# A decoder trunk on one core: its GEMM products read activations and write PSUM from the last column down, with row and weight splits placed anew by stage

## The chip, the cores and the metric

The kernel runs on one core of a Trainium2 chip. The metric is device time in microseconds (us) for one launch, as the median of the runs. Beside the runs there is one profiled execution, whose trace gives the start and the duration of every instruction on every engine: TensorE (PE, with weight loads as PEld), VectorE (DVE), ScalarE (ACT), GpSimd (POOL) and SyncE (SP).

## What is computed

The reference is a two-layer decoder trunk on 16 learned prefix tokens and 256 input tokens, so T = 272 columns of 2048 features, all in fp32:

```
h = concat(meta, x)                                   # 272 x 2048
a = rms_norm(h, norm_attn[0]);  q, k, v, f = split(a @ fox_w_in)
h = h + forgetting_attention(q, k, v, cumsum(log_sigmoid(f + b))) @ fox_w_o
h = h + square(relu(rms_norm(h, norm_mlp[0]) @ w_up[0])) @ w_down[0]
k, v = split(rms_norm(h, kv_norm) @ w_kv)             # layer 1 from here
q = rms_norm(h, norm_attn[1]) @ sb_w_q
h = h + stick_breaking_attention(q, k, v) @ sb_w_o
h = h + square(relu(rms_norm(h, norm_mlp[1]) @ w_up[1])) @ w_down[1]
return rms_norm(h, final_norm)[16:]
```

The MLPs are 2048 to 8192 to 2048. Of layer 1 only the 256 input tokens reach the output, so from its query projection on (the shared keys and values apart) the products need 256 columns and not 272.

## The kernel before, in words

Activations are held feature-major: features on the 128 partitions, 16 chunks of them, tokens along the columns. A product takes a 128x128 block of weights as the stationary operand and 272 or 256 columns of activations as the moving one, and adds to a PSUM tile `acc`.

To reach fp32 accuracy with the faster fp32r products, both operands are split into two fp32r parts, value = hi + lo, and each product is made three times: weight hi by row hi, weight hi by row lo, weight lo by row hi.

- `Split` (line 121) is the tile of one stage's split activations. A chunk has 640 elements per partition; hi and lo rows lie in it at two offsets taken from `ROWS` (line 27): 48 and 368 for 272 columns (t0 = 0), 0 and 320 for 256 columns (t0 = 16). Where t0 is not 0 it also defines `wide`, the hi rows with 6 columns more, and fills these with zeros by a POOL copy (line 135). ScalarE writes hi, VectorE lo (lines 137 to 142, 639 to 642).
- `weights` (line 201) loads a block of 512 output features by 512 input features in two DMAs of 512 KB on the SP queue, and splits it: ScalarE writes `whi` (line 225), VectorE `wlo` (line 226). Its argument `o1` is the element offset of the split weights in their tile, 0 for 272 columns and 16 for 256. The tiles hold 576 elements per chunk.
- `gemm_group` (line 230) makes 512 output features from all 2048 inputs: four weight blocks (kb), four input chunks in each (kc), four PSUM tiles (m) and three products: 192 products. `evac` then reads each PSUM tile. In `products` the 256-column order is pair, chunk, tile, the 272-column order tile, chunk, pair.
- In the 256-column stages three products of every fourth group (the list `wide`, line 261, with an own list for group 90) take `sp.wide`: 262 columns in place of 256, the 6 extra ones zero and never read.
- `gemm_matmul` (line 190) ties each product of the groups behind the one before it, so that the scheduler keeps their order.

The stages in order: 12 groups for q, k, v of layer 0 (`x_a0`), 4 for its output projection (`x_o0`), then four times 4 groups up (`x_m0`) and 4 groups down (`x_u0_f`); layer 1 has 4 groups for q (`x_a1`), 8 for keys and values (`x_kv`, 272 columns), 4 for the output projection (`x_o1`), and 16 up (`x_m1`) and 15 down (`x_u1_f`); the last block of 512 output features is made token-major by `token_group`, which the change does not touch. That is 56 groups at 272 columns and 39 at 256. Attention lies between the groups; its products (lines 435, 508, 603, 735, 757 and others) read some of the same splits (`x_o0`, `x_o1`) forward.

All tiles of splits begin at multiples of 64 elements.

Of the kernel before, what the change touches and what calls it, by code (L numbers as in the profile page):

```python
# [15 lines left out]
P = 128  # L16
D = 2048
NC = D // P
# [6 lines left out]
N_FF = 4  # L25

ROWS = {0: (48, 368), M: (0, 320)}
XROW = 640

G_A0, G_M0, G_KV, G_A1, G_M1, G_FIN = range(6)  # L30
# [3 lines left out]
def yoco_kernel(ctx: ExitStack, tc: tile.TileContext, hT_in, gains, b_f, w_f, w_qkv0, w_o0, w_up, w_dn,  # L34
                w_kv, w_q1, w_o1, g_row, out):
    nc = tc.nc
# [78 lines left out]
    pad = align.tile([P, 32], F32, name="pad")  # L115
# [5 lines left out]
    class Split:  # L121


        def __init__(self, label, t0):
            n = T - t0
            self.t0 = t0
            rows = xs.tile([P, NC * XROW + 64], F32R, tag="x", name=f"x_{label}")
            hi, lo = ROWS[t0]
            rows = rows[:, hi:hi + NC * XROW].rearrange("p (c t) -> p c t", c=NC)
            d = lo - hi  # L130
            self.hi, self.lo = rows[:, :, :n], rows[:, :, d:d + n]
            if t0:

                self.wide = rows[:, :, :n + 6]
                nc.gpsimd.tensor_copy(rows[:, :, n:n + 6], pad[:, :6].unsqueeze(1).to_broadcast([P, NC, 6]))

    def split_chunk(sp, gi, c):

# [47 lines left out]
    def behind(ins, other):  # L186
        tc.add_manual_dep(ins.ins, other.name, mybir.DependencyInfo(mybir.DependencyClass.NoSync,
                                                                    mybir.DependencyReason.DATA))

    def gemm_matmul(*args, **kw):  # L190

        ins = nc.tensor.matmul(*args, **kw).ins  # L192
        if queued and pinned[0]:
            tc.add_manual_dep(ins, queued[0].name, mybir.DependencyInfo(mybir.DependencyClass.NoSync,
                                                                        mybir.DependencyReason.DATA))
        queued[:] = [ins]
        if len(issued) == 192:
            issued.clear()
        issued.append(ins)

    def weights(u, kb, wblk, o1, load_x=None):

        src_w = wblk[kb].rearrange("p (k c) -> p k c", k=4)
        piece = 1 if load_x is not None and kb < 2 else 2
        raws = [wraw.tile([P, 2, 512], F32, tag="raw", name=f"raw_{u}_{kb}_{hf}") for hf in range(2)]
        for k0 in range(0, 4, piece):
            if load_x is not None:
                load_x(range(4 * kb + k0, 4 * kb + k0 + piece))
            if load_x is not None and kb == k0 == 0:

                for c0 in (0, 256):
                    nc.scalar.dma_start(raws[0][:, 0, c0:c0 + 256], src_w[:, 0, c0:c0 + 256])
            else:
                nc.sync.dma_start(raws[k0 // 2][:, k0 % 2:k0 % 2 + piece], src_w[:, k0:k0 + piece])
        parts = []
        for hf in range(2):
            whi, wlo = (wspl.tile([P, 2, 576], F32R, tag=f"w{x}", name=f"w{x}_{u}_{kb}_{hf}") for x in ("hi", "lo"))
            whi, wlo = whi[:, :, o1:o1 + 512], wlo[:, :, o1:o1 + 512]
            boxes = [(o, piece, 0, 512) for o in range(0, 2, piece)]
            if load_x is not None and kb == hf == 0:  # L220
                boxes[:1] = [(0, 1, 0, 256), (0, 1, 256, 512)]
            for o, no, c0, c1 in boxes:
                src = raws[hf][:, o:o + no, c0:c1]
                hp, lp = whi[:, o:o + no, c0:c1], wlo[:, o:o + no, c0:c1]
                on_act = nc.scalar.activation(hp, src, AF.Copy)  # L225
                on_dve = nc.vector.tensor_tensor(out=lp, in0=src, in1=hp.bitcast(F32), op=ALU.subtract)  # L226
            parts.append((whi, wlo))
        return parts, on_act, on_dve

    def gemm_group(wblk, sp, t0, evac, before={}, after={}, load_x=None):  # L230

        uid[0] += 1
        u = uid[0]
        accs = [pacc.tile([P, 512], F32, tag="acc", name=f"acc_{u}_{m}") for m in range(4)]
        n = T - t0
        for kb in range(4):
            if kb in before:
                before[kb]()  # L240
            parts, on_act, on_dve = weights(u, kb, wblk, 16 if t0 else 0, load_x)
            if kb in after:
                with tc.issue_after(on_act.ins), tc.issue_after(on_dve.ins):
                    after[kb]()

            if load_x is not None and kb == 0:
                runs = [([kc], range(4)) for kc in range(4)]
            elif kb in (0, 3):
                runs = [(range(4), [m]) for m in range(4)]
            else:  # L250
                runs = [(range(2 * hf, 2 * hf + 2), range(4)) for hf in range(2)]
            pinned[0] = load_x is None
            for kcs, ms in runs:
                pairs = ((0, sp.hi), (0, sp.lo), (1, sp.hi))
                if t0:
                    products = [(kc, m, *pair) for pair in pairs for kc in kcs for m in ms]
                else:
                    products = [(kc, m, *pair) for m in ms for kc in kcs for pair in pairs]
                left = {m: 3 * len(kcs) for m in ms}

                wide = [(0, 0, 0), (1, 0, 1), (2, 1, 1)] if t0 and u % 4 == 1 else []
                if u == 90:

                    wide = [(0, 0, 0), (0, 0, 1), (0, 2, 1)]
                for kc, m, part, x in products:
                    first, left[m] = kb == kc == 0 and left[m] == 3 * len(kcs), left[m] - 1
                    nw = n
                    if m == (0 if u == 90 else 3) and x is sp.hi and (kb, kc, part) in wide:
                        x, nw = sp.wide, n + 6
                    gemm_matmul(accs[m][:, :nw], parts[kc // 2][part][:, kc % 2, m * P:(m + 1) * P], x[:, 4 * kb + kc],  # L270
                                start=first, stop=kb == kc == 3 and left[m] == 0)
                if kb == 3:
                    for m in ms:
                        evac(m, accs[m][:, :n])
# [187 lines left out]
    for g in range(4):  # L462
# [11 lines left out]
        if g == 0:  # L474

            gemm_group(w_qkv0[0], xa, 0, lambda m, acc, qT=qT: nc.scalar.copy(qT[:, m, :], acc),
                       after={kb: (lambda kb=kb: first_norm(kb)) for kb in range(4)}, load_x=load_x)
# [12 lines left out]
        def decays(j):  # L490

            for i, (o, n) in enumerate(((0, 144), (144, T))):
# [5 lines left out]
                   after={j: (lambda j=j: decays(j)) for j in range(4)})  # L498
# [125 lines left out]
    def mlp(layer, xm, norm, t0, last_evac, last_group=None):  # L624
        box = {}

        def get_rstd():
            box["r"] = norm.finish()

        for f in range(N_FF):  # L630
            u = Split(f"u{layer}_{f}", t0)
            for g in range(4):
                def evac(m, acc, g=g):
                    c = 4 * g + m
                    r = tmp.tile([P, T], F32, tag="relu", name=f"relu_{layer}_{f}_{c}")
                    u2 = tmp.tile([P, T], F32, tag="u2", name=f"u2_{layer}_{f}_{c}")
                    nc.vector.scalar_tensor_tensor(out=r[:, t0:], in0=acc, scalar=0.0, in1=box["r"][:, t0:],
                                                   op0=ALU.max, op1=ALU.mult)
                    nc.scalar.activation(u2[:, t0:], r[:, t0:], AF.Square)
                    nc.scalar.activation(u.hi[:, c], u2[:, t0:], AF.Copy)  # L640
                    nc.vector.tensor_tensor(out=u.lo[:, c], in0=u2[:, t0:], in1=u.hi[:, c].bitcast(F32),
                                            op=ALU.subtract)
                gemm_group(w_up[layer, f, g], xm, t0, evac, {2: get_rstd} if f == g == 0 else {})
                if last_group is not None and f == N_FF - 1 and g == 0:
                    to_token_major()
            for g in range(4):
                def evac(m, acc, g=g):
                    residual_add(4 * g + m, acc, t0)
                    if f == N_FF - 1:
                        last_evac(4 * g + m)  # L650
                if last_group is not None and f == N_FF - 1 and g == 3:
                    last_group(w_dn[layer, f, g], u)
                else:
                    gemm_group(w_dn[layer, f, g], u, t0, evac)

    xm, norm_m = out_proj(w_o0, ao, 0, G_M0, "m0")
# [18 lines left out]
    for g in range(4):  # L675
# [4 lines left out]
        def split_c(kb, g=g):  # L680
            for c in ([4 * kb + g - 1] if g < 3 else [4 * kb + 2, 4 * kb + 3]):
# [3 lines left out]
                   after={kb: (lambda kb=kb: split_c(kb)) for kb in range(4)} if g else {})  # L685

    ao = Split("o1", M)
    for g in range(4):
# [12 lines left out]
        kc = packed(kT[:, :, 240:T], f"kc_{g}")  # L701
# [109 lines left out]
    xm, norm_m = out_proj(w_o1, ao, M, G_M1, "m1")  # L811
# [28 lines left out]
    def last_group(wblk, u):  # L840
        ob = xs.tile([P, NC * XROW + 64], F32, tag="x", name="ob")[:, :2 * D].rearrange("p (b d) -> p b d", b=2)

# [108 lines left out]
```

## Time and profile before

| what | value |
|---|---|
| median of 2 runs | 2282.02 us (2281.52 to 2282.51) |
| span of the profiled execution | 2278.5 us |
| median less span | 3.5 us |
| mean granted TensorE clock | 0.999 |
| TensorE products in the trace | 18,898 |
| data moved by DMA | 425.19 MB, 187 GB/s on average |

The profile gives for the profiled execution the span from its first to its last instruction; that is its own time here, and the runs' time lies 3.5 us above it. Products on TensorE overlap: one begins before the last one's modelled end. So a product's mean duration is no measure of what it costs; the distance between the starts of two products that follow each other is, and it is read off the timeline, where instructions of one kind that follow each other stand in one row with their count. A group of rows in the profile names line, engine, operation, the tile written and the tiles read, the shape, and the count. "wlo" and "whi" among the tiles read tell which part of the weights a product took.

### The profile page before, as it was taken

The page shows a single profiled execution, that of the slowest core. Times are in us where ns is not written, and L with a number is a line of the kernel's source. Part 1 is how long each engine was busy: PE and PEld are TensorE (multiplying, and loading weights), DVE is VectorE, ACT ScalarE, POOL GpSimd, SP SyncE. Part 2 cuts the span into 40 slices and gives each one's busy share as a digit, 9 for nine tenths or more (in the row PEclk, how much of TensorE's full clock was granted, in tenths as well). Part 3 has the DMA queues.
Part 4 walks back from the last instruction along what each step waited for, and adds up shares of the span by engine and source line. Part 5 has one row for each costly group of instructions (what it writes and reads, how often), then busy time and mean ns, then how long its engine had stood idle before and what let it go on. Part 6 is the DMA issues. An engine that isn't in the chain of part 4 may idle for free.

```text
span 2278.5 us, 44956 instructions
## 1 busy us (share of the span) xinstructions
PE 2271.1 (100%) x18898; PEld 2262.8 (99%) x18898; DVE 1333.5 (59%) x1930; ACT 1065.1 (47%) x1471; POOL 39.4 (2%) x72
## 2 busy tenths in 40 slices
PE   9999999999999999999999999999999999999998
PEld 9999999999999999999999999999999999999998
DVE  7767566554455455455566666666555555555555
ACT  6444445443354344335445555555443544543554
POOL 1000000000000000000000000000000000000001
PEclk9999999999999999999999999999999999999999
DMA  7765665555555555555556555555656556566564
GB/s 238 228 198 188 222 184 176 181 172 180 182 176 185 167 185 179 174 185 169 186 183 193 168 174 169 167 185 190 202 187 201 192 189 201 184 200 195 186 201 141
DMA packets 146171, 425.19 MB, mean 187 GB/s; under 512 B 31648, under 2 KB 43824, under 8 KB 145968
## 3 DMA queue, kind: packets, MB, share of 16 engines
q1 hardware_dynamic: 113760, 406.29, 54.1%
q10 hardware_dynamic: 32208, 16.02, 2.6%
q8 instruction: 148, 2.42, 0.4%
q14 instruction: 55, 0.45, 0.1%
HBM read 413.85 MB, written 8.41 MB: 185 GB/s over the span
## 4 chain that ended last, share of the span: by engine, by line
PE 99%; DMA 0%; issue 0%; POOL 0%; SPq 0%; POOLq 0%; ACT 0%; DVE 0%
PE acc L192 97%; PE po L435 0%; PE ps L435 0%; PE pza L435 0%; DMA raw<-w_qkv 0%; PE pzb L735 0%; PE po L804 0%; PE ps L508 0%; PE po L603 0%; PE pf L354 0%; PE pta L757 0%; PE pta L756 0%; PE pv L394 0%; POOL ob L850 0%; PE ptb L709 0%
## 5 line engine op out<-in xcount | busy, mean ns | idle before, releaser
L226 DVE TENSOR_TENSOR wlo<-raw,whi 128x1024 fp32r<-128x1024 f32 (+1 forms) x773 | 928.5, 1216 | 715.6 <-ACT whi L225 706.6
L225 ACT ACTIVATE whi<-raw 128x1024 fp32r<-128x1024 f32 (+1 forms) x773 | 796.4, 1050 | 961.0 <-PE acc L192 913.4
L192 PE MATMUL acc<-x_m,whi 128*128 128x272 f32 (+1 forms) x4096 | 643.1, 282 | 0.0
L192 PE MATMUL acc<-x_u,whi 128*128 128x272 f32 (+1 forms) x3968 | 626.0, 282 | 0.0
L192 PEld LDWEIGHTS acc<-x_m,whi 128*128 128x128 f32 x4096 | 566.0, 188 | 0.1
L192 PEld LDWEIGHTS acc<-x_u,whi 128*128 128x128 f32 x3968 | 550.4, 188 | 0.0
L192 PE MATMUL acc<-x_m,wlo 128*128 128x272 f32 (+1 forms) x2048 | 441.4, 282 | 0.0
L192 PE MATMUL acc<-x_u,wlo 128*128 128x272 f32 (+1 forms) x1984 | 432.1, 282 | 0.0
L192 PE MATMUL acc<-x_a,whi 128*128 128x272 f32 (+1 forms) x2048 | 355.4, 286 | 0.2 <-ACT whi L225 0.2
L192 PEld LDWEIGHTS acc<-x_m,wlo 128*128 128x128 f32 x2048 | 323.5, 188 | 0.0
L192 PEld LDWEIGHTS acc<-x_u,wlo 128*128 128x128 f32 x1984 | 315.3, 188 | 0.0
L192 PEld LDWEIGHTS acc<-x_a,whi 128*128 128x128 f32 x2048 | 301.3, 189 | 1.7 <-ACT whi L225 1.1
L192 PE MATMUL acc<-x_a,wlo 128*128 128x272 f32 (+1 forms) x1024 | 253.8, 286 | 0.0
L192 PE MATMUL acc<-x_kv,whi 128*128 128x272 f32 x1024 | 191.7, 288 | 0.0
L192 PEld LDWEIGHTS acc<-x_a,wlo 128*128 128x128 f32 x1024 | 175.7, 188 | 0.7 <-DVE ssq_a L158 0.4
L192 PE MATMUL acc<-x_o,whi 128*128 128x272 f32 (+1 forms) x1024 | 163.1, 283 | 0.0
L192 PEld LDWEIGHTS acc<-x_kv,whi 128*128 128x128 f32 x1024 | 160.1, 189 | 0.1
L192 PE MATMUL acc<-x_kv,wlo 128*128 128x272 f32 x512 | 147.6, 288 | 0.0
L192 PEld LDWEIGHTS acc<-x_o,whi 128*128 128x128 f32 x1024 | 142.3, 188 | 0.0
L307 DVE TENSOR_TENSOR hT<-acc,hT 128x272 f32<-128x272 f32 (+1 forms) x156 | 67.3, 431 | 75.4 <-PE acc L192 75.2
L192 PE MATMUL acc<-x_o,wlo 128*128 128x272 f32 (+1 forms) x512 | 110.7, 282 | 0.0
L192 PEld LDWEIGHTS acc<-x_kv,wlo 128*128 128x128 f32 x512 | 96.6, 189 | 0.0
(255 smaller groups left out, 1065.5 us busy)
## 6 DMA issues: line engine op xcount, KB each, us to landing
raw<-w_up SPq DMA_DIRECT2D x256, 512.0 KB, 3.9
raw<-w_dn SPq DMA_DIRECT2D x256, 512.0 KB, 4.0
raw<-w_qkv SPq DMA_DIRECT2D x92, 512.0 KB, 4.3
raw<-w_o SPq DMA_DIRECT2D x64, 512.0 KB, 3.9
raw<-w_kv SPq DMA_DIRECT2D x64, 512.0 KB, 4.4
raw<-w_q SPq DMA_DIRECT2D x32, 512.0 KB, 4.7
p_dram<-raw_p ACTq DMA_DIRECT2D x32, 96.0 KB, 4.6
v_dram<-turned ACTq DMA_DIRECT2D x48, 64.0 KB, 3.8
```

The costliest lines, as they stand in the source:

```text
L192: ins = nc.tensor.matmul(*args, **kw).ins
L225: on_act = nc.scalar.activation(hp, src, AF.Copy)
L226: on_dve = nc.vector.tensor_tensor(out=lp, in0=src, in1=hp.bitcast(F32), op=ALU.subtract)
L307: nc.vector.tensor_tensor(out=hT[:, c, t0:], in0=acc, in1=hT[:, c, t0:], op=ALU.add)
```

## The change

Three things are done, all in the products of `gemm_group` and in the places of their operands.

1. Every product of `gemm_group` reads its activation columns from the last to the first, and writes PSUM from the last column to the first. Each column's sum lands where it did. Weights are still loaded forward, and everything else reads and writes forward.
2. hi and lo rows of a stage lie at offsets of its own (`ROWS_OF`), and the weights of the up projections at 0, 16, 32 or 48 by the quarter f of the MLP. `x_m1` isn't in the table and keeps 0 and 320. The other weights keep 0 and 16.
3. The widened products and the zero fill of their extra columns are gone.

```diff
+ROWS_OF = {"a0": (0, 320), "o0": (16, 336), "m0": (32, 352), "u0_0": (0, 320), "u0_1": (0, 336), "u0_2": (0, 352),
+           "u0_3": (0, 368), "a1": (16, 336), "kv": (32, 368), "o1": (32, 352), "u1_0": (0, 320), "u1_1": (0, 336),
+           "u1_2": (0, 352), "u1_3": (0, 368)}
...
-            hi, lo = ROWS[t0]
+            hi, lo = ROWS_OF.get(label, ROWS[t0])
...
-            if t0:
-
-                self.wide = rows[:, :, :n + 6]
-                nc.gpsimd.tensor_copy(rows[:, :, n:n + 6], pad[:, :6].unsqueeze(1).to_broadcast([P, NC, 6]))
...
+    def backward(a):
+
+        *outer, (step, n) = a.ap
+        return bass.AP(a.tensor, a.offset + (n - 1) * step, [*outer, (-step, n)])
...
-    def gemm_group(wblk, sp, t0, evac, before={}, after={}, load_x=None):
+    def gemm_group(wblk, sp, t0, evac, before={}, after={}, load_x=None, shift=None):
...
-            parts, on_act, on_dve = weights(u, kb, wblk, 16 if t0 else 0, load_x)
+            parts, on_act, on_dve = weights(u, kb, wblk, shift if shift is not None else 16 if t0 else 0, load_x)
...
-                wide = [(0, 0, 0), (1, 0, 1), (2, 1, 1)] if t0 and u % 4 == 1 else []
-                if u == 90:
-
-                    wide = [(0, 0, 0), (0, 0, 1), (0, 2, 1)]
...
-                    nw = n
-                    if m == (0 if u == 90 else 3) and x is sp.hi and (kb, kc, part) in wide:
-                        x, nw = sp.wide, n + 6
-                    gemm_matmul(accs[m][:, :nw], parts[kc // 2][part][:, kc % 2, m * P:(m + 1) * P], x[:, 4 * kb + kc],
+                    gemm_matmul(backward(accs[m][:, :n]), parts[kc // 2][part][:, kc % 2, m * P:(m + 1) * P], backward(x[:, 4 * kb + kc]),
...
-                gemm_group(w_up[layer, f, g], xm, t0, evac, {2: get_rstd} if f == g == 0 else {})
+                gemm_group(w_up[layer, f, g], xm, t0, evac, {2: get_rstd} if f == g == 0 else {}, shift=16 * f)
```

## The prediction

> **What bounds the kernel now.** I read the page first: share of busy time, clock, and the chain that ended last.
>
> ```profile
> span 2278.5 us, 44956 instructions
> PE 2271.1 (100%) x18898; PEld 2262.8 (99%) x18898; DVE 1333.5 (59%) x1930; ACT 1065.1 (47%) x1471; POOL 39.4 (2%) x72
> PEclk9999999999999999999999999999999999999999
> PE 99%; DMA 0%; issue 0%; POOL 0%; SPq 0%; POOLq 0%; ACT 0%; DVE 0%
> ```
>
> TensorE is busy for all but 7 us at full clock, and the chain is 99% TensorE. The view of waits, for TensorE alone, says what it ever waited for:
>
> ```profile
> PE idle L61 <- DVE mean_w L57: 1.1, 1, 1.1
> PE pr_fin L192 <- DVE fin L863: 0.8, 1, 0.8
> PE acc L192 <- ACT whi L225: 0.2, 1, 0.2
> ```
>
> That is 2.1 us in all. So the time is the number of products times the distance from one product's start to the next: its pace. Durations (about 280 ns) overlap and say nothing here. The chain in order of time gives the pace of two long, undisturbed pieces:
>
> ```profile
> 427.93 756.83 PE acc L192 x6144
> 1581.78 533.37 PE acc L192 x4704
> ```
>
> The first piece is layer 0's MLP (272 columns): 756.83/6144 = 123.2 ns. The second is layer 1's MLP (256 columns): 533.37/4704 = 113.4 ns. The code has 56 groups of 192 products at 272 columns (10,752) and 39 at 256 (7,488, of which 33 are widened to 262, so 7,455). At these paces they make 1325 + 849 = 2174 us of the 2278.5. One nanosecond of pace is worth 10.8 us on the first kind and 7.5 us on the second.
>
> The pace isn't a constant of the shape. The timeline shows two values of it. First 256 columns, at the entry to three stages (query projection, output projection 1, MLP 1):
>
> ```profile
> 1186.94 1.11 PE L192 MATMUL acc<-x_a,wlo 128*128 128x256 f32 x8
> 1187.88 1.99 PE L192 MATMUL acc<-x_a,whi 128*128 128x256 f32 x16
> 1189.71 1.07 PE L192 MATMUL acc<-x_a,wlo 128*128 128x256 f32 x8
> 1190.62 1.07 PE L192 MATMUL acc<-x_a,whi 128*128 128x256 f32 x8
> ...
> 1493.99 2.05 PE L192 MATMUL acc<-x_o,whi 128*128 128x256 f32 x16
> 1495.88 1.11 PE L192 MATMUL acc<-x_o,wlo 128*128 128x256 f32 x8
> 1496.82 2.00 PE L192 MATMUL acc<-x_o,whi 128*128 128x256 f32 x16
> 1498.66 1.07 PE L192 MATMUL acc<-x_o,wlo 128*128 128x256 f32 x8
> 1499.57 0.62 PE L192 MATMUL acc<-x_o,whi 128*128 128x256 f32 x4
> ...
> 1583.50 1.11 PE L192 MATMUL acc<-x_m,wlo 128*128 128x256 f32 x8
> 1584.45 1.99 PE L192 MATMUL acc<-x_m,whi 128*128 128x256 f32 x16
> 1586.28 1.07 PE L192 MATMUL acc<-x_m,wlo 128*128 128x256 f32 x8
> 1587.18 1.07 PE L192 MATMUL acc<-x_m,whi 128*128 128x256 f32 x8
> ```
>
> Subtract starts. In the output projection, 24 products take 1496.82 - 1493.99 = 2.83 us, 117.9 ns each; the eight wlo products of the next turn take 1499.57 - 1498.66 = 0.91 us, 113.8 ns each. The other two stages do the same: eight in 0.94 and 0.95 us, then eight in 0.91 and 0.90 us. What lies at the switch? By form, the last stretch before it holds one widened product in each of the three stages:
>
> ```profile
> L192 PE MATMUL acc<-x_a,wlo 128*128 128x262 f32 x1 | 0.3, 284 | 0.0
> ...
> L192 PE MATMUL acc<-x_o,wlo 128*128 128x262 f32 x1 | 0.3, 283 | 0.0
> ...
> L192 PE MATMUL acc<-x_m,wlo 128*128 128x262 f32 x1 | 0.3, 285 | 0.0
> ```
>
> Nothing else differs in the code there. So at 256 columns the stream has a slow pace (117.9) that keeps itself up and a fast one (113.4) that does too, and a widened product seems to throw it from the one into the other: three stages of three. At 272 columns there are two paces as well; a stretch of the first products, then one of the MLP:
>
> ```profile
> 72.92 0.29 PE L192 MATMUL acc<-x_a,wlo 128*128 128x272 f32 x1
> ...
> 80.90 0.29 PE L192 MATMUL acc<-x_a,wlo 128*128 128x272 f32 x1
> ```
> ```profile
> 699.97 0.28 PE L192 MATMUL acc<-x_m,wlo 128*128 128x272 f32 x1
> ...
> 701.82 0.29 PE L192 MATMUL acc<-x_u,wlo 128*128 128x272 f32 x1
> ```
>
> A wlo product comes every third: 7.98 us for 63 products is 126.7 ns, 1.85 us for 15 is 123.3 ns. Here the slow pace ended without help.
>
> **The change part by part.** The instruction lists differ in nothing but seven POOL fills, the 33 products' width, and operands' addresses and direction: no instruction moves, no DMA or queue order changes, no wait is added.
>
> *Seven fills gone (line 135).* The pads of the widened products, on POOL:
>
> ```profile
> L135 POOL CAST x_u<-pad 128x96 fp32r<-128x96 f32 x4 | 1.1, 267 | 612.1 <-PE acc L192 612.1
> L135 POOL CAST x_m<-pad 128x96 fp32r<-128x96 f32 x1 | 0.5, 482 | 26.1 <-PE acc L192 26.1
> ```
>
> Under half a microsecond each, on an engine that is busy 2% and 0% of the chain: nothing. Without that cover all seven would be about 2 us.
>
> *Widened products gone.* Directly this saves 33 x 6 columns; at 113.4/256 = 0.44 ns a column, 0.1 us. Indirectly it removes what ended the slow pace. If layer 1's stages enter slow as they do now and nothing ends it, 7,455 products pay 117.9 - 113.4 = 4.5 ns: +33.5 us. If reading backward has no such slow pace: 0. Those are the ends. I take +33.5, since three entries of three were slow and each ended only with a widened product.
>
> *Other places of rows and weights.* Splits (ScalarE hi, VectorE lo) write as many elements at another offset. The weight splits already run at offset 0 in layer 0 and 16 in layer 1, with the same mean (first row from 500 to 1100 us, second from 1600 to 2200 us):
>
> ```profile
> L226 DVE TENSOR_TENSOR wlo<-raw,whi 128x1024 fp32r<-128x1024 f32 x203 | 245.1, 1223 | 244.9 <-ACT whi L225 244.9
> ...
> L226 DVE TENSOR_TENSOR wlo<-raw,whi 128x1024 fp32r<-128x1024 f32 x221 | 265.8, 1223 | 203.3 <-ACT whi L225 198.6
> ```
>
> So nothing, under TensorE's cover; eight of them are 9.8 us in a group that takes TensorE 192 x 113.4 = 21.8 us. For the products it may matter. Every stride between chunks is a multiple of 64 elements, so what a placement sets is the offset modulo 64. Now weights lie 16 elements past the rows in both shapes: rows 48, weights 0 at 272 columns; 0 and 16 at 256. The change gives 272 columns distances of 0 (qkv), -16 (output projection), -32 (kv) and -32 to 16 (up), and lets hi and lo part by up to 48 in the down projections. Only 4 of 56 groups keep the old distance, and 19 of 39 at 256 columns (by hi). No row shows a group at another distance, so the price goes by the two paces: between 0 and 126.7 - 123.3 = 3.4 ns on 10,752 products, +36.6 us; a gain is not excluded, since nobody's distance need be the best. I take 0, the row of most groups: the slow stretch at 272 columns ended by itself.
>
> *Backward.* Rows are read, and PSUM written, from the last column down; weights still load forward. No row of the trace has a negative step. Bounds: below, the closest thing to a stream limited by weight loads alone, the closing products of 128 columns:
>
> ```profile
> 2269.18 2.62 PE L192 MATMUL idle_fin<-mean_w 128*128 128x128 f32 x22
> ```
>
> The last lasts 0.275, so 21 starts in 2.345 us: 111.7 ns. At 256 columns that is -1.7 ns, -12.7 us. At 272 the shape has no lower row than 113.4 of the narrower one: -9.9 ns, -106 us. Above, both slow paces: +70 us together, already counted. I take 0 for the direction itself, in the middle, as the same columns stream.
>
> Sum against the profiled execution: 2278.5 - 0.1 + 33.5 = 2312 us of span. The runs' median is 2282.02, 3.5 us over the span, so 2315 us (+1.5%).
>
> **The rivals.**
> *B, the change does nothing to the pace*: descending order has one pace, and each stage stays at 123.3 and 113.4. Against it: the same instruction has two paces in this trace. For it: both values are locked over hundreds of microseconds. 2282 us. [...]
>
> *C, slow everywhere*: the scattered distances put 272 columns at 126.7 too. For it: a slow stretch of 63 products exists at the old distance. Against: it ended. 2315 + 36.6 = 2352 us (+3.0%). It passes 2% (about what a measurement of this kernel can tell from no change; 45.6 us) from a third of the 272-column products on, (45.6 - 33)/36.6.
>
> *D, faster*: moving rows and weights pass each other in opposite directions, so that they never run side by side and both slow and fast pace give way to a shorter one. It decides at a pace of 119.1 ns at 272 columns (45.6 us/10,752 = 4.2 ns off 123.3) with 256 unchanged. Bounds 2282 - 106 - 13 = 2163 us; halfway 2222. For it: 272 columns cost 9.8 ns more than 256, though 16 columns at 0.44 are 7.1, so there's slack of 2.7 ns at least. Against: no row shows it.
>
> *E, descending access isn't streamed at full rate*: at half rate all GEMM products double, some +2100 us. No row speaks to it; all operands there step forward by one. [...]
>
> **How the numbers follow.** A (2315) 0.34, B (2282) 0.13, C (2352) 0.29, D (2222) 0.17, E (over 4000) 0.07. Within 2%: A and B, 0.47. Slower: C and E, 0.36. Faster: D, 0.17. The likeliest case alone spans 2282 to 2328. For 8 in 10 I leave out E and the lower part of D: from 2220 to 2362 us, the top being C with 10 us for places worse than either pace.
>
> **What would show it.** In the changed profile: starts of wlo products in layer 1's long piece near 117.9 ns (A, C) or 113.4 (B); in layer 0's near 123.3 (A, B), 126.7 (C) or under 119 (D); differences between the four up projections of one layer would show that the places matter, none that only direction does. TensorE's waits should stay about 2 us. I am wrong if they grow, if a pace lies outside 111.7 to 117.9 at 256 columns or 113.4 to 126.7 at 272, or if the clock row falls below 9.

## The result and the profile after

The changed kernel takes 2332.7 us (median; 2332.16 to 2333.25) against 2282.02: 1.0226 times as long, interval 1.0207 to 1.0245. The span of its profiled execution is 2331.5 us, 53.0 more than before. The prediction said 2315, in a range of 2220 to 2362.

The page, same lines as before:

```profile
span 2331.5 us, 44923 instructions
PE 2322.9 (100%) x18898; PEld 2314.3 (99%) x18898; DVE 1335.5 (57%) x1930; ACT 1065.6 (46%) x1471; POOL 36.5 (2%) x65
PEclk9999999999999999999999999999999999999999
PE 99%; DMA 0%; issue 0%; POOL 0%; DVE 0%; SPq 0%; ACT 0%; POOLq 0%; ACTq 0%
```

TensorE makes as many products and is busy 51.8 us longer (2322.9 less 2271.1), at the same clock (1.000 on average against 0.999); VectorE and ScalarE are busy as long as before, within 2 us (1335.5 against 1333.5, 1065.6 against 1065.1). Its waits (engine, line, what it waited for, us in total):

```profile
PE idle L64 <- DVE mean_w L60: 1.1, 1, 1.1
PE pom L575 <- ACT vm_sb L573: 1.1, 1, 1.1
PE pr_fin L196 <- DVE fin L860: 0.8, 1, 0.8
PE acc L196 <- ACT whi L229: 0.4, 1, 0.4
```

That is 3.4 us in all, one wait of 1.1 us more than before. So it isn't waits that cost 53 us; the products follow each other more slowly. The chain in order of time (start, length, products), first three pieces of before that the prediction doesn't show, then the same five stretches after:

```profile
1185.22 104.29 PE acc L192 x899
1493.92 87.43 PE acc L192 x770
...
2116.02 138.64 PE acc L192 x1187
```
```profile
431.21 766.17 PE acc L196 x6144
1197.85 107.77 PE acc L196 x899
1511.76 92.23 PE acc L196 x770
1604.42 556.93 PE acc L196 x4704
2162.22 145.38 PE acc L196 x1187
```

Layer 0's MLP (x6144, 272 columns) grew by 766.17 - 756.83 = 9.3 us. The other four, mostly of 256 columns, grew by 3.5 + 4.8 + 23.6 + 6.7 = 38.6 us. The rest of the 53.0 lies in the shorter pieces between. Within one piece the pace isn't one number. The view by windows, for the GEMM line alone, with a window inside each of the four up projections of layer 0 and then of layer 1 (x counts the products; two of them began before the window):

```profile
445.00:510.00 65.00, 65.00 (x520) 1.00 0.55 179
613.00:703.00 90.00, 90.00 (x726) 1.00 0.57 182
805.00:895.00 90.00, 90.00 (x725) 1.00 0.56 182
997.00:1087.00 90.00, 90.00 (x722) 1.00 0.57 182
1618.00:1680.00 62.00, 62.00 (x527) 1.00 0.61 195
1777.00:1860.00 83.00, 83.00 (x707) 1.00 0.61 194
1960.00:2043.00 83.00, 83.00 (x694) 1.00 0.60 189
2187.00:2229.00 42.00, 42.00 (x352) 1.00 0.60 192
```

Length by count less two: 125.5, 124.3, 124.5 and 125.0 ns in layer 0, 118.1, 117.7, 119.9 and 120.0 ns in layer 1. The four stages of a layer run the same code and differ in the weights' offset only. So the places do matter, and none of these stages is at 123.3 or 113.3 any more.

### The profile page after: what moved, and what is told of

It reads as the page before. It is cut to its first block, busy times and chain, and to the rows that moved or that the text cites. A ratio compares the mean times of both kernels' runs of the same rounds, so it can differ in the third digit from the quotient of the medians.

```text
span 2331.5 us, 44923 instructions
## 1 busy us (share of the span) xinstructions
PE 2322.9 (100%) x18898; PEld 2314.3 (99%) x18898; DVE 1335.5 (57%) x1930; ACT 1065.6 (46%) x1471; POOL 36.5 (2%) x65
## 4 chain that ended last, share of the span: by engine, by line
PE 99%; DMA 0%; issue 0%; POOL 0%; DVE 0%; SPq 0%; ACT 0%; POOLq 0%; ACTq 0%
PE acc L196 96%; PE po L432 0%; PE ps L432 0%; PE pza L432 0%; DMA raw<-w_qkv 0%; PE pzb L732 0%; PE po L801 0%; PE ps L505 0%; PE po L600 0%; PE pf L351 0%; DMA v_dram<-turned 0%; PE pta L754 0%; PE pta L753 0%; PE pv L391 0%; POOL ob L847 0%
## 5 line engine op out<-in xcount | busy, mean ns | idle before, releaser
L196 PE MATMUL acc<-x_m,whi 128*128 128x272 f32 (+1 forms) x4096 | 659.1, 285 | 0.0
L196 PE MATMUL acc<-x_u,whi 128*128 128x272 f32 (+1 forms) x3968 | 639.7, 285 | 0.0
L196 PEld LDWEIGHTS acc<-x_m,whi 128*128 128x128 f32 x4096 | 577.5, 188 | 0.1
L196 PEld LDWEIGHTS acc<-x_u,whi 128*128 128x128 f32 x3968 | 559.3, 188 | 0.0
L196 PE MATMUL acc<-x_m,wlo 128*128 128x272 f32 (+1 forms) x2048 | 448.7, 285 | 0.0
L196 PE MATMUL acc<-x_u,wlo 128*128 128x272 f32 (+1 forms) x1984 | 437.4, 285 | 0.0
```

## The experiments

Three theories were set against each other. P: at 256 columns there are two self-sustaining paces, and the widened products end the slow one. D: falling access costs by itself. O: what counts is the distance of rows and weights. For D two halves were told apart later: R, the order in which rows are read, and W, the order in which PSUM is written. In the diffs, `...` marks lines not shown. The kernel before, run beside the experiments, had medians of 2280.6 to 2280.7 us; ratios are against these runs.

**Widened products and their fills taken out, nothing else.**

```diff
-            if t0:
-
-                self.wide = rows[:, :, :n + 6]
-                nc.gpsimd.tensor_copy(rows[:, :, n:n + 6], pad[:, :6].unsqueeze(1).to_broadcast([P, NC, 6]))
...
-                wide = [(0, 0, 0), (1, 0, 1), (2, 1, 1)] if t0 and u % 4 == 1 else []
...
+                wide = []
...
```

> The kernel before without its 33 widened products and their zero fills; forward, old places. Theory P (two self-sustaining paces at 256 columns, and a widened product is what ends the slow one): the 256-column stages stay at 117.9 ns from their entry on, 272 columns stay at 123.3; about +33 us, 2315. Theory D (descending access costs, widening is idle): 113.4 and 123.3 stay, 2282. Theory O (the distance of rows and weights costs): 2282.

2286.46 us, 1.0024 times before (1.0013 to 1.0035): +5.9 us and not +33. The chain:

```profile
428.31 756.82 PE acc L188 x6144
1185.59 107.15 PE acc L188 x899
1497.17 90.69 PE acc L188 x770
1588.29 533.14 PE acc L188 x4704
```

The pieces of the query projection (107.15 against 104.29) and of the output projection (90.69 against 87.43) are slow in all their 256-column products: 90.69/770 is 117.8 ns. P is right there. But MLP 1 (533.14) is as fast as before with no widened product in it. What ends the slow pace there is a break in its first group, where the norm's two products (line 159 here) come in between; ahead of it:

```profile
1586.75 1.10 PE L188 MATMUL acc<-x_m,wlo 128*128 128x256 f32 x8
1587.69 0.59 PE L159 MATMUL pms_m<-ssq_m,mean_w 128*128 128x256 f32 x2
```

Eight products take 0.94 us, 117.5 ns; behind the break the piece of 4,704 has 113.3. In the kernel before, the stream came to this break fast (eight wlo products from 1580.27 us on in 0.91 us, 113.8 ns) and left it slow (15 products from 1581.73 on in 1.77 us, 117.8 ns), and was fast again behind a widened product (eight in 0.90 us, in the prediction's rows). So one and the same break left the stream fast in one kernel and slow in the other. The norm's two products are one of plain fp32 in the code; they take 0.43 us of the chain of before, where an fp32r product takes 0.113 to 0.118:

```profile
1581.35 0.43 PE pms_m L163 x2
```

The prediction's other slow stretches of the kernel before also begin behind a break, and none of them where its stage begins. Ahead of the query projection's break the kernel before is fast:

```profile
1183.69 1.07 PE L192 MATMUL acc<-x_a,wlo 128*128 128x256 f32 x8
1184.60 0.62 PE L163 MATMUL pms_a<-ssq_a,mean_w 128*128 128x272 f32 x2
```

Eight products take 0.91 us, 113.8 ns each; behind the break come the prediction's 117.9. In the output projection the attention's products (lines 394, 435, 802 and 804) are the break: ahead of them 19 products from 1484.04 us on take 2.16 us, 113.7 ns, behind them eight from 1489.07 on take 0.94 us, 117.5 ns. At 272 columns, too, the slow stretch from 69 to 81 us begins behind two attention products (line 435, at 69.00; the three products from 68.50 on still take 0.37 us, 123.3 ns each) and ends at two others:

```profile
81.41 0.27 PE L552 MATMUL pm<-ident,s 128*128 128x128 f32 x1
81.51 0.27 PE L553 MATMUL pm<-ident,pk_sm 128*128 128x128 f32 x1
...
81.88 0.29 PE L192 MATMUL acc<-x_a,wlo 128*128 128x272 f32 x1
...
82.25 0.29 PE L192 MATMUL acc<-x_a,wlo 128*128 128x272 f32 x1
```

From one of these wlo rows to the next three products take 0.37 us, 123.3 ns each. So that pace didn't end without help, as the prediction has it: a break ended it.

**Backward at the old places.**

```diff
-            hi, lo = ROWS_OF.get(label, ROWS[t0])
+            hi, lo = ROWS[t0]
...
-                gemm_group(w_up[layer, f, g], xm, t0, evac, {2: get_rstd} if f == g == 0 else {}, shift=16 * f)
+                gemm_group(w_up[layer, f, g], xm, t0, evac, {2: get_rstd} if f == g == 0 else {})
```

> The changed kernel with the old places: backward, no widened products. Theory P: 256 columns at 117.9, 272 columns at 123.3, 2315. Theory D: as the changed kernel, 118 to 120 and 124.4 to 125.4, about 2333. Theory O: 113.4 and 123.3, 2282.

2329.03 us, 1.0210 (1.0180 to 1.0240).

```profile
431.54 767.31 PE acc L196 x6144
...
1604.62 554.03 PE acc L196 x4704
```

767.31/6144 = 124.9 ns, 554.03/4704 = 117.8 ns, the same in nearly all groups of a width. Against the run without widened products (2286.46) direction alone costs 42.6 us. D holds: it alone comes near at both widths. O falls as the sole cause, and P's 123.3 at 272 columns fails.

**Backward at the old places, widened products kept.**

```diff
-                    gemm_matmul(accs[m][:, :nw], parts[kc // 2][part][:, kc % 2, m * P:(m + 1) * P], x[:, 4 * kb + kc],
+                    gemm_matmul(backward(accs[m][:, :nw]), parts[kc // 2][part][:, kc % 2, m * P:(m + 1) * P], backward(x[:, 4 * kb + kc]),
```

> The kernel before with rows read and PSUM written backward, old places, widened products kept (the six zero columns come first). Theory P: the widened products end the slow pace here too, 113.4 after each; 2282 if direction is free. Theory D: 256 columns stay at 118 or above and 272 at 124.4 or above in spite of them, about 2333. Theory O: 2282.

2329.77 us, 1.0213 (1.0184 to 1.0243).

```profile
431.95 767.32 PE acc L197 x6144
...
1605.11 554.07 PE acc L197 x4704
```

The 33 widened products change nothing (2329.77 against 2329.03 us), and P's 113.4 behind each of them fails. Read backward, the stream has, as far as these runs go, one pace at this distance: 117.8 ns at 256 columns, the number of the slow one forward, and 125.0 at 272 through the stretch from 69 to 81 us too, where the forward stream is at 126.7. So P's two paces are seen in the forward read alone.

**The new places, forward, without and with widened products.** The first is the changed kernel with `backward` left out; the second is the kernel before with the table of places and the weights' offsets.

```diff
-                    gemm_matmul(backward(accs[m][:, :n]), parts[kc // 2][part][:, kc % 2, m * P:(m + 1) * P], backward(x[:, 4 * kb + kc]),
+                    gemm_matmul(accs[m][:, :n], parts[kc // 2][part][:, kc % 2, m * P:(m + 1) * P], x[:, 4 * kb + kc],
```

> The changed kernel reading and writing forward: new places, no widened products. Theory P: 256 columns at 117.9 in every stage, 272 at 123.3, 2315. Theory D: 2282 and no stage off its old pace. Theory O: paces that differ by stage, 118 to 120 and 124 to 126 where the distance is not the old one; about 2333, and the old paces where it is (up projections of the last quarter in layer 0, of the second in layer 1).

> Forward, the new places, widened products kept. Theory P (two self-sustaining paces at 256 columns where weights lie 16 elements past the rows): the down projections of the first quarter and the up projections of the second in layer 1, at 117.8 without widened products, come to 113.33 with them; the other stages, at other distances, stay as they were without; about 7 us under the run of places alone, some 2329. If the widened products do nothing for them: 2336.

2336.26 us, 1.0242 (1.0212 to 1.0271), and 2329.76 us, 1.0215 (1.0186 to 1.0245). Places alone cost about as much as direction alone (2336.26 and 2329.03 us), and the two don't add: both together are the changed kernel, 2332.70. The widened products are worth 6.5 us here, as P had it, and it lies in the two MLP stages of layer 1 where hi and lo are both at distance 16 (weights' offset less rows' offset). In layer 1's down projection of the first quarter, without them and with them:

```profile
1699.99 2.05 PE L196 MATMUL acc<-x_u,whi 128*128 128x256 f32 x16
1701.88 1.10 PE L196 MATMUL acc<-x_u,wlo 128*128 128x256 f32 x8
1702.82 0.40 PE L196 MATMUL acc<-x_u,whi 128*128 128x256 f32 x2
```
```profile
1699.95 1.98 PE L195 MATMUL acc<-x_u,whi 128*128 128x256 f32 x16
1701.77 1.07 PE L195 MATMUL acc<-x_u,wlo 128*128 128x256 f32 x8
1702.67 0.50 PE L195 MATMUL acc<-x_u,whi 128*128 128x256 f32 x3
```

24 products take 2.83 us (117.9 ns) and 2.72 us (113.3 ns), at the same places and in the same direction. This is the cleanest sight of the two paces. Both streams enter the stage slow; by the starts in the trace, the second turns from 117.8 to 113.3 ns right behind its first product of 262 columns, at 1695.84 us.

These runs, with the kernel before, the changed kernel and the backward ones, also give the pace by distance (taken modulo 64 elements). The numbers are mean times in ns from one start to the next, over undisturbed groups behind a stage's first one, hi and lo at equal offsets:

| distance | 272 forward | 272 backward | 256 forward | 256 backward |
|---|---|---|---|---|
| 16 | 123.33 (126.67 in the stretch at 69 us) | 125.00 | 113.33 or 117.78 | 117.78 |
| 0 | 125.33 | 124.44 | 120.00 | 118.33 |
| 32 | 126.67 | 125.33 | 118.67 | 120.00 |
| 48 | 126.67 | 124.44 | 117.78 | 120.00 |

Where a distance occurs at two places, the pace is the same: at 272 columns 16 with rows 48 and weights 0, and with rows 32 and weights 48; at 256 columns 0 with both at 0 and both at 16, in either direction. O is right in that distance and direction set the pace together. No cell is under the fast one of the kernel before. The cells of 126.67 may be a second pace that was entered, as is seen for distance 14 below; no run tells for these.

The table holds only where hi and lo lie at equal distances. Where they don't, the pace needn't be a mean of the two cells: layer 0's down projection of the third quarter (hi at 0, lo at 32) runs forward at 124.44 ns, below both, and that of the second quarter (hi at 0, lo at 48) backward at 125.19, above both. Why is open.

**Only the read, only the write backward.** Two kernels at the old places, without widened products: one has `backward` around the rows alone, the other around PSUM alone. Each product's columns land in reversed order, so neither computes the reference; number and shape of the products are the same. The first one's edit, against the changed kernel:

```diff
-                    gemm_matmul(backward(accs[m][:, :n]), parts[kc // 2][part][:, kc % 2, m * P:(m + 1) * P], backward(x[:, 4 * kb + kc]),
+                    gemm_matmul(accs[m][:, :n], parts[kc // 2][part][:, kc % 2, m * P:(m + 1) * P], backward(x[:, 4 * kb + kc]),
```

> As the backward kernel at the old places without widened products, but only the rows are read from the last column; PSUM is written forward, so each product's columns land in reversed order and the output is another one. Theory R (the order in which rows are read against the weight loads sets the pace): 125.0 ns at 272 and 117.8 at 256 columns, about 2329. Theory W (the falling order of PSUM writes costs): 123.33 and 113.33 with the first two 256-column stages at 117.8, about 2286.

> The counterpart: rows are read forward and only PSUM is written from the last column, so each product's columns land in reversed order and the output is another one. Theory R: 123.33 and 113.33, with the query and output projection of layer 1 at 117.8, about 2286. Theory W: 125.0 and 117.8, about 2329.

2329.23 us, 1.0213 (1.0183 to 1.0243), for the read; 2287.01 us, 1.0027 (1.0016 to 1.0038), for the write. The two long pieces, read then write:

```profile
432.29 767.31 PE acc L196 x6144
...
1605.38 554.03 PE acc L196 x4704
```
```profile
428.65 756.82 PE acc L196 x6144
...
1588.62 533.14 PE acc L196 x4704
```

The first has the pieces of the wholly backward run to the last digit, the second those of the forward run without widened products. R is shown, at these places: all of it is the reading of rows; writing PSUM in falling order costs nothing that can be seen (2287.01 against 2286.46 us).

**Order of blocks, order inside blocks.** Old places, no widened products, rows and PSUM in blocks of 16 columns (64 bytes).

```diff
-        return bass.AP(a.tensor, a.offset + (n - 1) * step, [*outer, (-step, n)])
+        return bass.AP(a.tensor, a.offset + n - 16, [*outer, (-16, n // 16), (1, 16)])
```

and `a.offset + 15, [*outer, (16, n // 16), (-1, 16)]` for the other.

> Old places, no widened products; rows are read and PSUM is written in blocks of 16 columns, the blocks from the last to the first, the columns inside a block rising. Theory B (what counts is the order in which the read passes blocks of 64 bytes while weights load): as wholly backward, 125.0 and 117.8, about 2329. Theory I (falling order of single elements counts): as forward without widened products, 123.33 and 113.33 but for the query and output projection of layer 1, about 2286. Any other pace: the two-step pattern has a price of its own.

> The counterpart: blocks of 16 columns from the first to the last, the columns inside a block falling. Theory B: as forward without widened products, about 2286. Theory I: as wholly backward, about 2329.

2369.98 us, 1.0390 (1.0360 to 1.0421), for falling blocks; 2606.17 us, 1.1426 (1.1393 to 1.1459), for falling columns inside rising blocks. The long pieces of the one and of the other:

```profile
443.26 790.82 PE acc L196 x6144
...
1645.54 554.03 PE acc L196 x4704
```
```profile
478.74 859.52 PE acc L196 x6144
...
1790.94 627.19 PE acc L196 x4704
```

Falling blocks give 117.8 ns at 256 columns, as wholly backward, but 128.7 at 272; falling columns in rising blocks 133.3 and 139.9. Neither theory has these: the two-step pattern has prices of its own, so the pair doesn't settle which order the direction works through. Nor does it tell whether the prices lie in the read or in the write, as both take the pattern here.

**Finer distances.** The kernel before with other weights' offsets in the MLPs, in two runs: up projections 8, 12, 20, 24 and down projections 4, 28, 14, 18 by quarter; then up projections 20, 24, 14, 18 and every down projection at 16.

```diff
+            self.first = hi
...
-            parts, on_act, on_dve = weights(u, kb, wblk, 16 if t0 else 0, load_x)
+            parts, on_act, on_dve = weights(u, kb, wblk, (sp.first + far) % 64, load_x)
...
```

> The kernel before (forward, widened products) with distances between 16 and its neighbours on the grid of 16 elements: up projections 8, 12, 20, 24 by quarter, down projections 4, 28, 14, 18. Theory O (pace is a function of direction and of the distance of rows and weights modulo 64): each value has one pace for its width, the same in all four groups of the stage; those near 16 at 123.33 and 113.33, those near 0 and 32 at 125.3 and 118 to 120. If only blocks of 16 elements count, 20 and 24 go with 16; if there is a better place than 16, a pace under 123.33 or 113.33 shows it.

> The kernel before with up projections at distances 20, 24, 14, 18 by quarter and every down projection at 16. If 126.67 at 272 columns with 20 and 14 was carried over from the stage ahead (28), then 20 and 14 come to 123.33 here, as 18 and 24 did; if the distance sets it, they stay at 126.67 and each down projection is at 123.33 again. Layer 1: 118.7, 118.7, 117.8 and 118.3 as seen for these distances, and 113.33 for each down projection after its first widened products.

2323.92 us, 1.0190 (1.0160 to 1.0219), and 2298.92 us, 1.0079 (1.0050 to 1.0108). At 256 columns the paces went from 117.8 (14) and 118.3 (4, 8, 12, 18) over 118.7 (20, 24) to 120.0 (28); the four distances that both runs have agree within 0.2 ns, and only 16 gave 113.33. At 272 columns 12 gave 124.44; 18 and 24 gave 123.33 in both runs and 20 gave 126.67 in both, so the carrying over that was offered for 20 falls: in the second run the stage ahead ends at 123.3. O's two paces near 16 (123.33 and 113.33) are thus met in part only. For 14 the carrying over holds: a window inside its stage, first run, then second:

```profile
920.00:990.00 70.00, 70.00 (x555) 1.00 0.53 175
```
```profile
815.00:885.00 70.00, 70.00 (x570) 1.00 0.57 179
```

70 us by 553 and by 568 products (the counts less the two that began before): 126.6 and 123.2 ns. At this distance, too, 272 columns have two paces. No finer distance beats 16.

**Nine widened products in place of 33.** In the first group of the query projection, the output projection and MLP 1 only.

```diff
-                wide = [(0, 0, 0), (1, 0, 1), (2, 1, 1)] if t0 and u % 4 == 1 else []
...
+                wide = [(0, 0, 0), (1, 0, 1), (2, 1, 1)] if u in (49, 61, 65) else []
...
```

> The kernel before with widened products only in the first group of the query projection, of the output projection and of the MLP of layer 1 (nine in place of 33). Theory P (a pace keeps itself up once it's entered): 113.33 from there to the end, the same time as before, 2282. If each stage needs its own: 117.8 in later stages, up to 2305.

2280.13 us, 1.0000 (0.9988 to 1.0011), and the long piece of MLP 1:

```profile
1581.84 533.25 PE acc L192 x4704
```

As expected from P: the fast pace, once entered, lasts 533 us without help. No run of this case beat the kernel before beyond its interval.

## Why the prediction held in its number and not in its cause

The median lies 18 us over the forecast, and that nearness is luck: the term that made up the forecast is nearly empty, and one put at nothing took its place.

- *The bound.* Right. TensorE's stream of products sets the end before and after, and the change acts on its pace alone: as many products, the same clock, 3.4 us of waits.
- *The fills and six columns.* Nothing visible, as said; TensorE's own extra time is accounted for by pace.
- *Widened products gone, +33.5 us.* This is the step that failed. Taking them out costs 5.9 us. That a widened product ends the slow pace had been read correctly, and the query and output projection bear it out. But the three slow stretches were taken for the way in which a stage is entered; each begins behind a break, and I let three of them stand for all of layer 1's 39 groups. Without widened products the stream comes to MLP 1's break slow, not fast, and leaves it fast. Under backward reading widened products do nothing at all (2329.77 with, 2329.03 without).
- *Direction, 0.* Mis-sized, and at the old places it is the main term: 42.6 us, all of it from reading rows backward: +1.7 ns at 272 columns (125.00 less 123.33) and +4.4 at 256 (117.78 less 113.33). I chose the middle of bounds of -119 and +70 us with no row for it; that weight loads alone set the 111.7 ns of the lower bound was my estimate, and no run shows it. The nearest row for the direction was the slow pace of the same products, and that is what backward reading got at 256 columns. So the pace of 117.9 in layer 1 was forecast for the wrong reason, and came about by luck; 2315 lay 18 us under the result mostly because 272 columns were held at 123.3.
- *Places, 0.* Wrong for the places alone, forward (2336.26 us), and nearly right in the change itself, where rows are read backward: 2331.5 less 2327.1 of span against the old places, 4.4 us. The text's reason, that the slow stretch at 272 columns ended by itself, fails twice: it ended at a break, and it says nothing about other distances, which run forward at 125.3 to 126.7 through whole stages.
- *The rivals.* B falls by the first experiment on direction. C (slow at both widths, 2352) was nearer in kind: every 272-column stage is over 123.33, at 124.4 to 125.3, a third to three fifths of the way to 126.67. D falls: no distance that was run has a pace under 123.33 and 113.33 in either direction. E falls: backward throughout costs 42.6 us and not 2100.
- *The signs it named.* By these the mechanism is wrong: layer 1's stages run at up to 120.0 ns, outside 111.7 to 117.9, and TensorE's waits grew from 2.1 to 3.4 us, though these 1.3 us are little of the 53. The sign for the places, up projections of one layer that differ, did show.
- *Weights and PSUM.* The same products run at 113.33 to 120.00 ns at 256 columns as only the weights' offset changes (distances 16 and 28 in the runs of finer distances), and PSUM written in falling order isn't slowed (2287.01 against 2286.46 us).

Shown is that the direction in which rows are read and the distance of rows and weights set the pace together, and that forward the stream has two paces at distances 14 (123.2 and 126.6 ns at 272 columns) and 16 (113.33 and 117.78 at 256), and which of them it has depends on what ran before. Why this is so, none of these runs shows. The texts take weights as loaded forward, as the code's access pattern has them; the order in which a load passes its columns isn't seen in a trace, and a kernel with reversed weights wasn't tried.

## What to carry to other kernels

Where TensorE is busy throughout, divide time by products in a stage and compare stages: here 5 ns a product in layer 1's MLP (118.4 against 113.4) made 23.6 us and showed in no wait. When a stream has two self-sustaining paces, follow it to each break (another operation in between, a stage's entry) before counting a slow stretch for the whole of what comes behind it. And when a change turns several things at once, don't put an unknown one at nothing because that is the middle of its bounds: here direction alone made 2329.03 of the 2332.70 us, places alone 2336.26, and the two didn't add, so only runs with one part each tell them apart.

## What the hardware showed that was not expected

- The pace of fp32r products depends on the distance between the moving and the stationary operand modulo 64 elements, from 113.33 to 120.00 ns at 256 columns and from 123.33 to 126.67 at 272, and, at the pairs of places that were run, not on where the pair lies (forward, weights 48 below the rows and 16 above them both run at 123.33).
- One stream can hold either of two paces over whole stages (117.78 or 113.33 ns at distance 16 and 256 columns). Behind a product of 262 columns the slow one had become the fast one (117.8 and 113.3 ns in layer 1's first down projection); behind the norm's two products the stream ran at 113.3 after 117.5 ns in one kernel, at 117.8 after 113.8 in another.
- The pace depends on the direction of the read: at distance 0 backward is faster (124.44 against 125.33, 118.33 against 120.00), at 16 slower than the fast pace forward (125.00 against 123.33, 117.78 against 113.33).
- Falling order inside rising blocks of 16 columns, in read and write at once, costs far more than falling order throughout: 133.3 against 117.8 ns at 256 columns, 139.9 against 124.9 at 272.
